# A squared-ReLU MLP on eight cores: the down projection as seven block products in place of eight, with sums shared in PSUM

## The chip, the cores and the metric

The kernel runs on all 8 cores of one Trainium2 chip, one sequence of the batch on each core, with no communication between them. The metric is the device time of the slowest core, in microseconds (us). Some executions fell in a second, slower state: some or all cores of one die show a lower granted clock than the others, and the time is longer.

A word on the names. TensorE multiplies (PE in the profile; PEld is its weight load), VectorE (DVE), ScalarE (ACT) and GpSimd (POOL) work on the elements, SyncE (SP) issues transfers. TensorE writes into PSUM, which the kernel uses as eight banks of 128x512 fp32; its other tiles lie in SBUF. "L858" is line 858 of that kernel's source, and one source line keeps its meaning in all kernels, though its number moves.

## The reference, cut to what matters

```python
D_MODEL = 1024; BATCH = 8; SEQ = 2048; D_FF = 4 * D_MODEL
...
        # token-mixing sub-layer: attention in two groups of heads, with a rotary key (k_pe)
        h = rmsnorm(x, norm_mix_g[l]) * (1.0 + sc1) + sh1
        ...
        x = x + g1 * jnp.einsum('bse,ed->bsd', mix, w_o[l])
        # channel-mixing sub-layer: squared-ReLU MLP
        h = rmsnorm(x, norm_mlp_g[l]) * (1.0 + sc2) + sh2
        u = jnp.square(jax.nn.relu(jnp.einsum('bsd,df->bsf', h, w_up[l])))
        x = x + g2 * jnp.einsum('bsf,fd->bsd', u, w_down[l])
    return rmsnorm(x, final_g)
```

The last einsum is the down projection: 2048 tokens by 4096 hidden features by 1024 outputs on each core.

## The kernel before

The kernel records operations with the buffers that they read and write. Its own scheduler then puts them in an order for each engine, places the PSUM tiles in banks and adds the semaphores. So the order of the source isn't the order on the engine.

The MLP runs over 4 quarters `q` of the hidden width and 4 groups `G` of 512 tokens, 16 blocks in all. The up matmuls of the next block are recorded ahead of the down matmuls of this one:

```python
        def mm_group(out, bank, lhs_list, rhs_list, rbufs):
            n = len(lhs_list)
            for i in range(n):
                S.op("pe", lambda h, i=i: h.matmul(out, lhsT=lhs_list[i], rhs=rhs_list[i], start=(i == 0), stop=(i == n - 1)),
                     r=rbufs[i], w=[bankb[bank]])
...
        def load_dn(q, after=()):           # down weights: load fp32, scale by the gate, store bf16
            ...
                S.op("dve", lambda h, c=c, w_=w_: h.tensor_tensor(out=WDN[s_][:, c, :], in0=WST[w_], in1=G2B, op=ALU.mult),
                     r=[bWST[w_], bG2], w=[bWDN[s_][c]])
...
        def mlp_up(q, G, fcs=range(8), banks=(0, 1, 2, 3)):
            for fc in fcs:
                ...                         # 8 matmuls into one bank
                if (q == 0 and G < 2) or (q == 3 and fc % 2):
                    S.op("dve", ...tensor_scalar(out=RT[rs], in0=bk(b), scalar1=0.0, scalar2=None, op0=ALU.max)...)
                    S.op("pool", ...tensor_tensor(out=UT[us][:, fc, :], in0=RT[rs], in1=RT[rs], op=ALU.mult)...)
                else:
                    S.op("act", ...activation(out=RT[rs], in_=bk(b), func=AF.Relu)...)
                    S.op("act", ...activation(out=UT[us][:, fc, :], in_=RT[rs], func=AF.Square)...)
...
        def mlp_down(q, G):
            ...
            for j in range(4):              # 4 token tiles of the group
                t = G * 4 + j
                for half in range(2):       # 2 x 512 output features
                    b = take_bank((4, 5, 6, 7))
                    mm_group(bk(b), b, [UT[us][:, fc, j * 128:(j + 1) * 128] for fc in range(8)],
                             [WDN[s_][:, fc, half * 512:(half + 1) * 512] for fc in range(8)],
                             [[bUT[us][fc], bWDN[s_][fc]] for fc in range(8)])
                    ...                     # VectorE: X1[t] += bank (a copy in the first quarter)
```

Two small pieces of the earlier stage are touched as well. The rotary key is copied to 8 heads by DMA, and eight scalings of two columns are VectorE instructions:

```python
            S.op("dve", lambda h: h.tensor_tensor(out=KPE, in0=TQ[0:32, :], in1=TQ[32:64, :], op=ALU.add), r=[bTQ], w=[bKPE])
            for r0 in (64, 96):
                S.dma("sp", lambda h, r0=r0: h.dma_start(out=KG[G][r0:r0 + 32, :, :],
                                                         in_=KPE.unsqueeze(1).to_broadcast([32, 8, 512])), ...)
...
        def scale_cols(i, src, c):          # (1 + MODCOL) * gain, 128x2
            S.op("dve", lambda h: h.scalar_tensor_tensor(out=GCOLS[:, i, 2 * c:2 * c + 2], ..., scalar=1.0, ..., op0=ALU.add, op1=ALU.mult),
                 r=[bMOD[src // 2 + c], bPAR], w=[bGC[i][c]])
```

The softmax here doesn't subtract the row's maximum and nothing guards it: scores larger than these inputs give would overflow.

## Time and profile before

| kernel before | |
|---|---|
| time, first three runs | 868.8 us (867.95 to 871.31) |
| slowest core of the profiled run | 873.4 us |
| TensorE busy there | 800.3 us in 5674 matmuls |
| VectorE, ScalarE, GpSimd busy | 391.8, 412.7, 194.0 us |
| from 0 to 442 us (projections, attention, start of the MLP) | TensorE idle for 64 us |
| from 442 to 862 us (the rest of the MLP) | TensorE idle for 0 us |

How to read it: the busy share of TensorE, 92%, mixes two stages. In the second one only the number of matmuls counts. In the first, TensorE waits for others, and a matmul saved there may be worth nothing. The prediction shows the lines and works with them.

### The profile page before, as it was taken

The numbers are of one execution on the slowest core, as the hardware profiler recorded it, in microseconds if no ns is written. First come the engines' busy times: TensorE is split into PE (matmuls) and PEld (weight loads), VectorE is DVE, ScalarE is ACT, GpSimd is POOL, SyncE is SP. The second block draws the span as 40 slices with busy tenths as digits, with TensorE's granted clock in tenths as the row PEclk, the third lists the DMA queues.
The fourth block names the chain that finished last, engine by engine and source line by source line (L and its number), as shares of the span: only waits on it lengthen the run. The fifth ranks groups of instructions, "written<-read, shape, count | busy, mean of one in ns | idle before, by whom it ended". The sixth has DMA issues, their size and how long they took to land.

```text
span 873.4 us, 16095 instructions; the slowest of 8 cores (854.4 to 873.4 us)
## 1 busy us (share of the span) xinstructions
PE 800.3 (92%) x5674; PEld 412.3 (47%) x5674; DVE 391.8 (45%) x684; ACT 412.7 (47%) x670; POOL 194.0 (22%) x164
## 2 busy tenths in 40 slices
PE   0697978899999988997999999999999999999995
PEld 0353546566556655554444444444444444444442
DVE  2575635844543436665662222512215344325546
ACT  3328627467789895770204323442234322124434
POOL 2020127557954443100170000000000000111110
PEclk9998989999999998999999999999999999999999
DMA  9999761579214355886571050600505321002213
GB/s 183 239 157 181 153 140 39 112 134 196 69 26 168 112 170 128 238 277 205 144 173 46 1 96 1 188 6 1 97 1 168 121 97 49 1 1 96 82 64 144
DMA packets 34301, 98.33 MB, mean 113 GB/s; under 512 B 3376, under 2 KB 9648, under 8 KB 34096
## 3 DMA queue, kind: packets, MB, share of 16 engines
q1 hardware_dynamic: 26016, 69.91, 24.6%
q0 software_dynamic: 8208, 27.40, 19.5%
q8 instruction: 47, 0.77, 0.4%
q14 instruction: 30, 0.25, 0.1%
HBM read 102.67 MB, written 19.92 MB: 140 GB/s over the span
## 4 chain that ended last, share of the span: by engine, by line
PE 79%; DMA 10%; issue 3%; ACT 3%; DVE 3%; POOL 1%; SPq 0%; DVEq 0%; ACTq 0%; POOLq 0%
PE ps L844 64%; PE ps L1225 6%; DMA arena<-wada 4%; PE ps L1249 3%; DMA arena<-arena 3%; DMA arena<-wdn 2%; DMA arena<-x 1%; PE ps L1271 1%; PE ps L1296 1%; PE ps L936 1%; PE ps L1333 1%; ACT arena L1058 1%; ACT arena L1233 1%; DMA mxs<-arena 1%; PE ps L1413 1%
## 5 line engine op out<-in xcount | busy, mean ns | idle before, releaser
L844 PE MATMUL ps<-arena 128*128 128x512 bf16 (+3 forms) x3444 | 676.1, 346 | 47.2 <-DMA arena<-wada 22.5
L844 PEld LDWEIGHTS ps<-arena 128*128 128x128 bf16 (+1 forms) x3444 | 298.3, 98 | 372.3 <-issue 68.2
L1472 ACT ACTIVATE arena<-ps 128x512 f32<-128x512 f32 x96 | 57.4, 598 | 250.8 <-PE ps L844 250.5
L1233 ACT ACTIVATE arena<-ps 128x1024 bf16<-128x1024 f32 (+1 forms) x160 | 138.8, 897 | 57.8 <-PE ps L1249 28.6
L1603 DVE TENSOR_TENSOR arena<-ps,arena 128x512 f32<-128x512 f32 x104 | 70.9, 689 | 150.8 <-PE ps L844 150.5
L1225 PE MATMUL ps<-arena 128*128 128x512 bf16 (+3 forms) x416 | 88.4, 310 | 4.8 <-ACT arena L1233 3.3
L911 ACT ACTIVATE arena<-arena 128x1024 bf16<-128x1024 f32 x47 | 49.6, 1055 | 87.9 <-DVE arena L1603 35.5
L1469 POOL TENSOR_TENSOR arena<-arena 128x512 bf16<-128x512 f32 x32 | 35.2, 1111 | 251.5 <-DVE arena L1467 243.1
L1278 POOL TENSOR_TENSOR arena<-arena 128x1024 bf16<-128x1024 f32 x31 | 73.0, 2354 | 62.5 <-ACT arena L1275 34.4
L1249 PEld LDWEIGHTS ps<-arena 128*128 128x128 bf16 x1088 | 54.1, 98 | 27.6 <-issue 6.7
L1249 PE MATMUL ps<-arena 128*128 128x65 bf16 x1088 | 63.8, 195 | 3.6 <-DVE arena L1310 2.9
L1474 ACT ACTIVATE arena<-arena 128x512 bf16<-128x512 f32 x96 | 60.6, 631 | 9.4 <-ACT arena L1472 0.9
L1238 POOL TENSOR_TENSOR arena<-arena 128x512 bf16<-128x512 bf16 x32 | 37.9, 1184 | 72.6 <-ACT arena L1233 57.8
L1445 DVE TENSOR_TENSOR arena<-arena 128x1024 bf16<-128x1024 f32 x32 | 40.6, 1275 | 27.4 <-DMA arena<-wdn 26.9
L1435 POOL DMA_DIRECT2D arena<-wup x16 | 9.1, 578 | 169.7 <-PE ps L844 169.7
L1225 PEld LDWEIGHTS ps<-arena 128*128 128x128 bf16 x416 | 32.1, 99 | 25.1 <-issue 16.2
L1467 DVE TENSOR_SCALAR arena<-ps 128x512 f32<-128x512 f32 x32 | 21.9, 690 | 46.9 <-PE ps L844 42.4
L1600 DVE COPY arena<-ps 128x512 f32<-128x512 f32 x24 | 16.4, 689 | 46.4 <-PE ps L844 46.4
L1387 DVE TENSOR_TENSOR arena<-ps,arena 128x512 f32<-128x512 f32 x32 | 22.0, 688 | 31.1 <-PE ps L844 18.9
L1275 ACT ACTIVATE arena<-ps 128x1024 f32<-128x1024 f32 x31 | 31.7, 1024 | 7.4 <-PE ps L844 1.8
L868 POOL DMA_DIRECT2D arena<-wada x24 | 13.6, 571 | 87.5 <-PE ps L844 45.7
L1353 DVE TENSOR_TENSOR arena<-ps,arena 128x512 bf16<-128x512 f32 x32 | 21.9, 688 | 21.2 <-PE ps L844 12.9
(83 smaller groups left out, 460.9 us busy)
## 6 DMA issues: line engine op xcount, KB each, us to landing
arena<-x SPq DMA_DIRECT2D x32, 512.0 KB, 9.0
arena<-wdn SPq DMA_DIRECT2D x32, 512.0 KB, 4.5
arena<-wada POOLq DMA_DIRECT2D x24, 512.0 KB, 11.0
arena<-wup POOLq DMA_DIRECT2D x16, 512.0 KB, 7.2
out<-arena SPq DMA_DIRECT2D x15, 512.0 KB, 2.6
x1s<-arena SPq DMA_DIRECT2D x12, 512.0 KB, 5.0
arena<-x1s SPq DMA_DIRECT2D x12, 512.0 KB, 3.2
mxs<-arena SPq DMA_DIRECT2D x12, 256.0 KB, 2.2
```

The source lines that it names most:

```text
L844: S.op("pe", lambda h, i=i: h.matmul(out, lhsT=lhs_list[i], rhs=rhs_list[i], start=(i == 0), stop=(i == n - 1)), r=rbufs[i], w=[bankb[bank]])
L911: S.op("act", lambda h: h.activation(out=dst, in_=src, func=AF.Square, accum_out=STA[st][:, j:j + 1]), r=[bsrc], w=[bSTA[st][j], bdst])
L1225: S.op("pe", lambda h, c=c, j=j, q0=q0, n=n: h.matmul(score(t)[:, c:c + n], lhsT=KG[j // 4][:, hh, j % 4 * 128:j % 4 * 128 + 128], rhs=QG[ ...
L1233: S.op("act", lambda h: h.activation(out=PT[p][:, 0:n], in_=score(t)[:, 0:n], func=AF.Exp, scale=MLA_SCALE), r=[t.buf], w=[bPT[p]])
L1238: S.op("pool", lambda h: h.tensor_tensor(out=v, in0=v, in1=TRI.unsqueeze(1).to_broadcast([128, m, 128]), op=ALU.mult), r=[bPT[p], bTRI], w ...
L1249: sp=(self.last and i == len(blocks) - 1): h.matmul(bk(ob, None, (qb * 65, qb * 65 + 65)), lhsT=PT[p][:, c:c + 128], rhs=vaug(j, hh), star ...
L1278: S.op("pool", lambda h: h.tensor_tensor(out=PTS[ps], in0=PE32[p], in1=EM[:, idx, :].rearrange("p (a b) -> p a b", a=2, b=512), op=ALU.mul ...
L1445: S.op("dve", lambda h, c=c, w_=w_: h.tensor_tensor(out=WDN[s_][:, c, :], in0=WST[w_], in1=G2B, op=ALU.mult), r=[bWST[w_], bG2], w=[bWDN[s ...
L1469: S.op("pool", lambda h, rs=rs, fc=fc: h.tensor_tensor(out=UT[us][:, fc, :], in0=RT[rs], in1=RT[rs], op=ALU.mult), r=[bRT[rs]], w=[bUT[us] ...
L1472: S.op("act", lambda h, b=b, rs=rs: h.activation(out=RT[rs], in_=bk(b), func=AF.Relu), r=[bankb[b]], w=[bRT[rs]])
L1474: S.op("act", lambda h, rs=rs, fc=fc: h.activation(out=UT[us][:, fc, :], in_=RT[rs], func=AF.Square), r=[bRT[rs]], w=[bUT[us][fc]])
L1603: S.op("dve", lambda h, t=t, hs=hs, b=b: h.tensor_tensor(out=X1[t][:, hs], in0=bk(b), in1=X1[t][:, hs], op=ALU.add), r=[bankb[b], bX1[t]], ...
```

## The change

The intent: the down projection of a block, 512 tokens by 1024 hidden by 1024 outputs, is cut in 2x2 blocks on all three sides. Strassen's scheme (in Winograd's form, with shared sums) takes 7 block products in place of 8, for four sums of activation blocks and four sums of weight blocks. The products that several output blocks share add up in one PSUM bank: product 1 is read out (for output block 00), 6 is accumulated upon it and the sum read (01), then 7 (11), then 4 (10). So 14 readings serve a block.

```diff
+        def sub(d, a, b, op=ALU.subtract):
+            S.op("dve", lambda h: h.tensor_tensor(out=d[0], in0=a[0], in1=b[0], op=op), r=a[1] + b[1], w=d[1])
+        def t_comb(q):                      # 4 sums of weight blocks, once a quarter
+            sub(WT[0], B[0, 1], B[0, 0]); sub(WT[2], B[1, 1], B[0, 1]); sub(WT[1], B[1, 1], WT[0]); sub(WT[3], B[1, 0], WT[1])
+        def s_comb(i):                      # 4 sums of activation blocks, in each of 15 blocks
+            sub(USB[0], A[1, 0], A[1, 1], ALU.add); sub(USB[2], A[0, 0], A[1, 0]); sub(USB[1], USB[0], A[0, 0]); sub(USB[3], A[0, 1], USB[1])
...
         def mlp_down(q, G):
+            ...                             # q == 3 and G == 3: as before, 64 matmuls
+            prods = {1: (u_blk(us, 0, 0), B[0, 0]), 2: (u_blk(us, 0, 1), B[1, 0]), 3: (USB[3], B[1, 1]),
+                     4: (u_blk(us, 1, 1), WT[3]), 5: (USB[0], WT[0]), 6: (USB[1], WT[1]), 7: (USB[2], WT[2])}
+            chain = {1: "a", 6: "a", 7: "a", 4: "a", 5: "b", 3: "b", 2: "c"}
+            to = {1: (0, 0), 6: (0, 1), 7: (1, 1), 4: (1, 0), 5: (1, 1), 3: (0, 1), 2: (0, 0)}
+            for p, n in ((0, 1), (0, 5), (1, 1), (0, 6), (1, 5), (0, 2), (1, 6), (0, 7), (0, 3), (1, 2), (1, 7), (0, 4), (1, 3), (1, 4)):
+                key = (p, chain[n])
+                first = key not in banks    # a bank for each chain of each half
+                ...
+                for f in range(4):
+                    S.op("pe", ...matmul(bk(b), lhsT=av[:, f, ...], rhs=wv[:, f, :], start=(first and f == 0), stop=(f == 3))...)
+                r, half = to[n]
+                acc(q, 4 * G + p + 2 * r, half, b)      # VectorE: X1 += bank
```

Two companions come with it in the earlier stage. For the first two groups the rotary key is copied by VectorE in place of the DMA; and four of the eight column scalings go to GpSimd as two instructions each (computed as m*g + g):

```diff
+            if G < 2:
+                for r0 in (64, 96):
+                    S.op("dve", ...tensor_copy(out=KG[G][r0:r0 + 32, :, :], in_=KPE.unsqueeze(1).to_broadcast([32, 8, 512]))...)
+                return
...
+            if i == 0:
+                S.op("dve", ...scalar_tensor_tensor...)     # as before
+            else:
+                S.op("pool", ...tensor_tensor(out=gc, in0=mc, in1=g, op=ALU.mult)...)
+                S.op("pool", ...tensor_tensor(out=gc, in0=gc, in1=g, op=ALU.add)...)
```

The rest makes room: the down weights lie in four blocks and are scaled in halves of 512 columns, output tiles are tracked by halves, and the scratch for DMA descriptors is halved. Two smaller things move as well: the matmuls of the MLP's loop may take any of the eight banks (before, up and down had four each), and the gain of the last normalisation is loaded later.

## The prediction

> **What bounds the kernel now.** I read the page first, then the chain of waits in order of time, then busy time by windows, then the rows of single instructions. The page's first part says that TensorE is busy for 92% of the span and nothing else for more than half:
>
> ```profile
> PE 800.3 (92%) x5674; PEld 412.3 (47%) x5674; DVE 391.8 (45%) x684; ACT 412.7 (47%) x670; POOL 194.0 (22%) x164
> ```
>
> That share is an average over two different stages. The chain of waits has one piece that is nearly half of the span (start, length, what, how many instructions):
>
> ```profile
> 442.39 419.32 PE ps L844 x1942
> ```
>
> The windows, cut at that piece's ends (the columns are the stretch, its length, busy time with instruction counts of PE, PEld, DVE, ACT and POOL, then the granted clock, the DMA share and GB/s):
>
> ```profile
> 0.00:442.39 442.39, 378.35 (x3720) 221.17 (x3721) 231.10 (x482) 268.14 (x411) 161.28 (x129) 0.97 0.65 154
> 442.39:861.90 419.51, 419.51 (x1944) 190.29 (x1945) 154.42 (x195) 140.30 (x248) 32.73 (x35) 1.00 0.23 68
> 861.90:873.40 11.50, 2.39 (x12) 0.88 (x9) 6.29 (x9) 4.29 (x11) 0.00 (x0) 0.83 0.34 138
> ```
>
> From 442.39 to 861.90 us, the MLP, TensorE never stops: 419.51 busy of 419.51, at full clock. 419.32 us over 1942 matmuls is 0.2159 us each. Nothing but fewer matmuls can shorten this stage, and each one taken away is worth 0.216 us as long as no wait takes its place. VectorE works for 37% of it (154.42 of 419.51), so there is room for more work beside it. The stage before is another matter: TensorE idles 64 of 442 us there, and two of the idle stretches are touched by this change. The waits ahead of TensorE (in brackets: idle before, and who ended it), and the VectorE row behind the second:
>
> ```profile
> 122.80 1.04 PE L844 MATMUL ps<-arena 128*128 128x512 bf16 x3 [5.06 <-DVE arena L1047]
> 155.47 0.90 PE L844 MATMUL ps<-arena 128*128 128x512 bf16 x3 [4.26 <-DVE arena L940]
> 150.63 4.29 DVE L899 SCALAR_TENSOR_TENSOR arena<-arena 128x2 f32<-128x2 f32 x1
> 151.45 2.35 POOL L1278 TENSOR_TENSOR arena<-arena 128x1024 bf16<-128x1024 f32 x1
> ```
>
> The first comes from a copy of the rotary key by DMA: the chain has 23.77 us of "DMA arena<-arena" from 97.38 us on, and VectorE sits 10.3 us behind it. The second is an instruction on two columns that takes 4.29 us instead of its median of 0.16, beside a GpSimd instruction.
>
> [...] after the idle 5.06 us the granted clock reads 0.50 from 122 to 128 us, and 0.57 from 156 to 160. [...] 689 ns for the 512-column accumulation out of PSUM[...], 1226 ns for the median 1024-column fp32 scaling[...]. No bf16 SBUF-only addition runs on VectorE before the change[...]. [...]
>
> **The change part by part.**
>
> *Matmuls removed.* The down projection is 4 quarters of the hidden width by 4 groups of 512 tokens, 16 blocks of 64 matmuls. Fifteen become 7 products of 8 matmuls, 56; the last stays at 64. 15 x 8 = 120 fewer, x 0.2159 = **25.9 us**, all of it on the path. This is 2.98% of 868.8.
>
> *Readings added.* Each product is added from PSUM into its output tile while the bank goes on accumulating: 14 readings of 128x512 in a block where there were 8. 15 x 6 = 90 more at 0.689 = 62 us of VectorE.
>
> *Sums of blocks added.* Per Strassen block four sums of 128x1024 bf16 of the activations: 60 at an estimated [...] 0.69 us[...] = 41 us. Per quarter four sums of 128x2048 of the weights: 16 at 1.22 = 20 us. The scaling of the down weights is cut in halves, 64 at 0.69 in place of 32 at 1.23 to 1.27: +4 us. Together VectorE gains 127 us, and in the MLP goes from 154 to some 280 of 394 us, 71%. So VectorE doesn't become the bound by its sum.
>
> *Does it fit in time?* One step of the steady state is 64 up matmuls (13.8 us) and 56 down (12.1 us). In the 12.1 us VectorE has 14 x 0.69 = 9.7 us of readings. The listing of VectorE's order shows the sums for the next block standing between them: with all four, 12.4 us of work in 12.1. What doesn't fit runs on into the 13.8 us of up matmuls, where VectorE has little to do. A single bank is tighter. A product takes 4 x 0.216 = 0.86 us, and a bank is written again after two other products at the least, 1.73 us. The reading needs a semaphore each way (0.14 us between VectorE and TensorE in the chain at 122.66) and 0.69: about 1.0. That leaves 0.75 us: one activation sum ahead of the reading fits (0.69), a weight sum (1.22) makes TensorE wait 0.5. In five of the 15 blocks the listing of TensorE's order puts two up matmuls ahead of the last product, which fills 0.43 us of just such a wait. In each of the three blocks that end a quarter two weight sums stand between the readings, the others behind them: 6 x 0.5 = 3 us at most, some of it hidden where the bank read next has more room, and some lost elsewhere to queueing. I charge **+2.5** for the stage.
>
> *The start of the MLP.* From 420 to 470 us VectorE gains the first four weight sums (4.9), four activation sums (2.8), the split scalings and a dozen readings (8), and in the same stretch GpSimd squares the activations[...]. Before, TensorE already waits 1.6 us for those squares at 441. I charge **+4**.
>
> *The early stage.* For the first two groups the rotary copy moves from DMA to VectorE, where it is a few us of work in a stretch in which VectorE waits; the later four of the eight small column scalings move to GpSimd[...]. What can come back is 5.06 idle plus half of some 5.7 us at half clock (2.9), and 4.26 plus 0.43 x 4 = 1.7: 13.9 us. The instructions behind then meet the next limit, so I take less than half: **-6**. The halved descriptor scratch is needed for the space and I give it nothing.
>
> *The end.* The last block is unchanged and the 11.5 us after the last matmul hold the same chain; four output tiles of the group before are finished together and late: **+0.5**.
>
> Sum: 868.8 - 25.9 - 6 + 4 + 2.5 + 0.5 = 843.9.
>
> **The rivals.** *VectorE paces the down blocks.* For it: 12.4 us of work in 12.1 with the sums, 19 with the weight sums, a queue in strict order, and readings queued behind scalings that wait for a DMA (26.9 us of such waits in all now). Against it: the readings have 0.75 us of slack, and 13.8 us of up matmuls after each block take up what is left over. If each of 15 blocks lost 1 us more, 859, within 2%. *The early stage gives nothing*, because the DMA queue or ScalarE bounds it (ScalarE is busy 45.3 of 50 us from 250 on): 850, just beyond 2%. *The early stage gives all*: 836. *The clock falls under the denser work*: the MLP reads 1.00 throughout and TensorE is no denser than before; I leave it out. *Accumulating and reading in one bank serialises*: if every product waited for its own reading, 15 x 14 x 0.3 us or more, 63 us slower; the three chains of banks per half speak against it.
>
> **Range and chances.** The 25.9 is a count by a measured time and is firm to 1 us. The early stage is open by +6 or -6, the stalls from 0 to +10. Together 844, from 835 to 854 in 8 of 10. Faster by over 2% means under 851.4: 0.86. Slower needs over 40 us of new waits: 0.01.
>
> **What would show it.** In the changed profile: 1824 or so matmuls between the start of the dense piece and its end; if the step of 0.216 us holds, that piece lasts some 394 us, with waits of TensorE for VectorE below 5 us in sum and mostly in the blocks that end a quarter. Activation sums near 0.69 and weight sums near 1.22 us; VectorE near 280 us in the MLP. The 5.06 and 4.26 us waits gone, and the MLP starting some 6 us earlier than 442. I am wrong if TensorE has many waits near 0.5 us on the accumulation,[...] or if the idle time of the early stage only moves.

The forecast's sum came to 868.8 - 25.9 - 6 + 4 + 2.5 + 0.5 = 843.9. Its terms +4 and +2.5, and 61 of the 127 us of VectorE's gain, rest in part on 0.69 us for an activation sum (128x1024 bf16) and 1.22 us for a weight sum (128x2048). These were the assumption; the trace of the kernel before has no such sum. The changed kernel's trace has means of 0.708 and 1.214 us.

## The result, and the profile after

| | before | after |
|---|---|---|
| median | 870.05 us (867.95 to 871.64, 4 runs) | 839.88 us (838.73 to 841.27, 4 runs) |
| ratio, 95% interval | | 0.9655 (0.9624 to 0.9686) |

A ratio here is the mean time of one kernel's fast runs over that of the other's fast runs of the same rounds, so it isn't quite the ratio of the medians. 3.45% of 870.05 is 30.0 us. The point of the prediction, 844.0, was 4 us too high; the time lies in its range. The results of this kernel and of all that follow were correct.

The engines' busy line of the changed kernel, from its page (which is of core 0, 836.1 us; the views below are of core 3, 836.8 us):

```profile
PE 770.8 (92%) x5554; PEld 397.0 (47%) x5554; DVE 504.9 (60%) x882; ACT 409.7 (49%) x670; POOL 200.8 (24%) x172
```

The counts are those of the plan: 5674 - 5554 = 120 matmuls fewer, VectorE with 113 us more work (127 by the prediction's sum of durations). The chain of waits in the middle of the MLP of the changed kernel (core 3, span 836.8 us; start, length, what, how many):

```profile
464.14 12.09 PE ps L1682 x56
476.23 13.81 PE ps L858 x64
```

The chain runs through TensorE alone, here and in the blocks that follow: 56 matmuls of a down block (L1682) take 12.09 us, so 0.2159 us each, and the 64 up matmuls (L858) follow without a gap. The windows of the changed kernel, with the columns of the prediction's table; the first ends at the start of the MLP, the third is its even part:

```profile
0.00:408.40 408.40, 359.17 (x3653) 211.38 (x3654) 218.50 (x474) 267.77 (x411) 156.22 (x131) 0.98 0.65 153
408.40:463.00 54.60, 48.94 (x221) 21.34 (x219) 45.07 (x62) 7.86 (x13) 21.68 (x18) 0.97 0.54 141
463.00:814.00 351.00, 350.40 (x1623) 158.40 (x1622) 224.78 (x327) 122.95 (x216) 22.72 (x24) 1.00 0.22 65
```

In the third window TensorE is busy 350.40 of 351.00 us at a clock of 1.00, though VectorE now works 64% of the time there. The second window is the sore point: VectorE 45.07 of 54.60 us, TensorE idle for 5.7. The waits of TensorE behind the last transpose ahead of the MLP, which starts at 427.3 us in the kernel before and at 408.4 us in the changed one (who it waited for; us in sum, times, the longest), first of the kernel before, then of the changed one, core 3 of both:

```profile
PE ps L844 <- POOL arena L1469: 1.6, 1, 1.6
```

```profile
PE ps L1682 <- DVE arena L1607: 2.6, 1, 2.6
PE ps L1682 <- DVE arena L1643: 1.8, 1, 1.8
PE ps L1682 <- POOL arena L1495: 1.2, 1, 1.2
PE ps L1682 <- DVE arena L1645: 0.6, 2, 0.4
```

L1607 is a sum of blocks, L1643 and L1645 are readings of a bank (the first as a copy), L1495 is GpSimd's squares. In the changed kernel they come to 6.2 us on this core and to 6.9 to 9.3 us on the others. The first three all stand between 409 and 444 us: 5.6 to 7.3 us by core, 6.6 in the mean, where the kernel before has 0 to 1.6 us, 0.3 in the mean. The readings of the whole even part cost 0.6 us on this core and 0.3 to 2.0 on the others. So nearly all of the 120 matmuls turned into time, except at the start of the MLP.

### The profile page after: what moved, and what is told of

Its sections match the earlier page's. It is cut to its first block, busy times and chain, and to the rows that moved or that the text cites. A ratio compares the mean times of both kernels' runs of the same rounds, so it can differ in the third digit from the quotient of the medians.

```text
span 836.1 us, 16205 instructions; the slowest of 8 cores (829.1 to 836.8 us)
## 1 busy us (share of the span) xinstructions
PE 770.8 (92%) x5554; PEld 397.0 (47%) x5554; DVE 504.9 (60%) x882; ACT 409.7 (49%) x670; POOL 200.8 (24%) x172
## 3 DMA queue, kind: packets, MB, share of 16 engines
q1 hardware_dynamic: 24928, 68.87, 24.9%
## 4 chain that ended last, share of the span: by engine, by line
PE 81%; DMA 7%; DVE 4%; issue 3%; ACT 3%; POOL 1%; SPq 0%; DVEq 0%; ACTq 0%; POOLq 0%
PE ps L858 45%; PE ps L1682 21%; PE ps L1248 7%; PE ps L1272 4%; DMA arena<-winl 3%; DMA arena<-wdn 2%; PE ps L1294 1%; DMA arena<-x 1%; DMA arena<-wada 1%; PE ps L1319 1%; PE ps L1356 1%; DVE arena L1470 1%; PE ps L1436 1%; ACT arena L1256 1%; DVE arena L1645 1%
## 5 line engine op out<-in xcount | busy, mean ns | idle before, releaser
L858 PE MATMUL ps<-arena 128*128 128x512 bf16 (+3 forms) x2484 | 468.6, 331 | 29.8 <-DMA arena<-wada 21.7
L858 PEld LDWEIGHTS ps<-arena 128*128 128x128 bf16 (+1 forms) x2484 | 203.6, 98 | 240.3 <-issue 47.1
L1682 PE MATMUL ps<-arena 128*128 128x512 bf16 x840 | 188.4, 381 | 7.8 <-DVE arena L1643 3.3
L1645 DVE TENSOR_TENSOR arena<-ps,arena 128x512 f32<-128x512 f32 x194 | 127.3, 685 | 76.9 <-PE ps L1682 73.6
L1256 ACT ACTIVATE arena<-ps 128x1024 bf16<-128x1024 f32 (+1 forms) x160 | 138.5, 895 | 43.2 <-PE ps L1272 18.9
L1682 PEld LDWEIGHTS ps<-arena 128*128 128x128 bf16 x840 | 82.1, 98 | 109.2 <-issue 13.1
L1495 POOL TENSOR_TENSOR arena<-arena 128x512 bf16<-128x512 f32 x32 | 40.5, 1270 | 236.9 <-PE ps L858 125.2
L1248 PE MATMUL ps<-arena 128*128 128x512 bf16 (+3 forms) x416 | 87.7, 306 | 6.6 <-ACT arena L1256 4.9
L1272 PE MATMUL ps<-arena 128*128 128x65 bf16 x1088 | 65.7, 193 | 1.3 <-DVE arena L1282 0.3
L1272 PEld LDWEIGHTS ps<-arena 128*128 128x128 bf16 x1088 | 54.3, 97 | 25.3 <-issue 4.4
L1607 DVE TENSOR_TENSOR arena<-arena 128x1024 bf16<-128x1024 bf16 (+1 forms) x76 | 61.0, 815 | 0.6
L1470 DVE TENSOR_TENSOR arena<-arena 128x512 bf16<-128x512 f32 x64 | 48.2, 789 | 13.5 <-DMA arena<-wdn 10.9
L1248 PEld LDWEIGHTS ps<-arena 128*128 128x128 bf16 x416 | 31.6, 97 | 25.8 <-issue 16.9
L1410 DVE TENSOR_TENSOR arena<-ps,arena 128x512 f32<-128x512 f32 x32 | 22.0, 689 | 32.7 <-PE ps L858 15.0
L1298 ACT ACTIVATE arena<-ps 128x1024 f32<-128x1024 f32 x31 | 31.7, 1023 | 10.5 <-POOL arena L1301 3.8
```

The source lines that it names most:

```text
L1248: S.op("pe", lambda h, c=c, j=j, q0=q0, n=n: h.matmul(score(t)[:, c:c + n], lhsT=KG[j // 4][:, hh, j % 4 * 128:j % 4 * 128 + 128], rhs=QG[ ...
L1256: S.op("act", lambda h: h.activation(out=PT[p][:, 0:n], in_=score(t)[:, 0:n], func=AF.Exp, scale=MLA_SCALE), r=[t.buf], w=[bPT[p]])
L1272: sp=(self.last and i == len(blocks) - 1): h.matmul(bk(ob, None, (qb * 65, qb * 65 + 65)), lhsT=PT[p][:, c:c + 128], rhs=vaug(j, hh), star ...
L1470: S.op("dve", lambda h, c=c, w_=w_, n=n, v=v: h.tensor_tensor(out=v[:, c % 4, :], in0=WST[w_][:, n * 512:n * 512 + 512], in1=G2B[:, n * 51 ...
L1607: S.op("dve", lambda h: h.tensor_tensor(out=d[0], in0=a[0], in1=b[0], op=op), r=a[1] + b[1], w=d[1])
L1645: S.op("dve", lambda h: h.tensor_tensor(out=X1[t][:, hs], in0=bk(b), in1=X1[t][:, hs], op=ALU.add), r=[bankb[b], bX1[t][half]], w=[bX1[t][ ...
```

## The experiments

Twelve kernels ran in three batches, each batch on one chip with the kernel before beside it. The questions: (a) how the gain divides between the matmuls and the two companions; (b) why TensorE waits at the start of the MLP; (c) how near VectorE is to becoming the bound; (d) what the sharing of banks and the order of products are worth.

### (a) Companions and matmuls apart

**early_only** is the kernel before with both companions, **rope_only** and **scale_only** have one each, and **strassen_only** is the changed kernel with both taken back:

```diff
 # strassen_only, against the changed kernel
-            if G < 2:
-                ...tensor_copy(out=KG[G]...)   # back to the DMA
-                S.op("pool", ...)              # scale_cols: back to VectorE
```

> The kernel before with the two companions alone (rotary copy of groups 0 and 1 by VectorE, the second set of column scalings on GpSimd), no Strassen. Theory A, from the two traces: the companions bring 12 to 15 us, because the last transpose ahead of the MLP ends 14.5 us earlier in the median core; expects 855 to 858, ratio near 0.984. Theory B: the earlier mark is work that moved, and Strassen alone brings the whole 30 us; expects 866 to 870, ratio 0.995 to 1.0.

> The changed kernel with both companions put back (rotary copies by DMA, all column scalings on VectorE). Theory A: 25.9 us of matmuls less some 8 of waits at the start of the MLP, 17 to 19 us; expects 851 to 853, ratio near 0.980. Theory B: 840 to 843, ratio near 0.967.

> The kernel before with the rotary copy of groups 0 and 1 by VectorE alone. Theory A: takes the 5.1 us wait of TensorE at 122.8 and the half-speed clock behind it, 7 to 9 us; expects 861 to 863. Rival: the attention starts earlier but meets the stuck column scaling, which then costs more; expects 866 to 870.

> The kernel before with the second set of column scalings on GpSimd alone. Theory A: takes the 4.3 us wait at 155.5 and its clock loss, 5 to 6 us; expects 864 to 866. Rival: the 4.29 us instruction was slow in this one profile by chance, nothing comes back; expects 869 to 871.

| kernel | median | ratio to before (95%) | about |
|---|---|---|---|
| early_only | 860.84 us | 0.9879 (0.9860 to 0.9898) | -10.5 us |
| strassen_only | 852.32 us | 0.9763 (0.9729 to 0.9796) | -20.6 us |
| rope_only | 867.78 us | 0.9961 (0.9942 to 0.9979) | -3.4 us |
| scale_only | 864.74 us | 0.9916 (0.9892 to 0.9940) | -7.3 us |

(us: one minus the ratio, times 870. The median of strassen_only is over six runs of which two were slow; its fast runs lie from 848.16 to 854.64. early_only and scale_only had one slow run each.) The parts multiply: 0.9879 x 0.9763 = 0.9645 against 0.9655 for the whole change, and 0.9961 x 0.9916 = 0.9877 against 0.9879. By the expectations, strassen_only and scale_only came out as theory A says, rope_only in its rival's range, and early_only between its two theories.

So a third of the gain isn't Strassen's. The waits of TensorE between 100 and 300 us suggest why the smaller companion gave more. The three longest entries of the kernel before, then those of rope_only, scale_only and early_only that are over 2 us (for the last, which has none, its longest):

```profile
PE ps L844 <- DVE arena L1047: 5.1, 1, 5.1
PE ps L844 <- DVE arena L940: 4.3, 1, 4.3
PE ps L844 <- DVE arena L1336: 1.2, 1, 1.2
```

```profile
PE ps L844 <- DVE arena L940: 4.3, 1, 4.3
PE ps L844 <- DVE arena L1341: 2.1, 1, 2.1
```

```profile
PE ps L844 <- DVE arena L1051: 3.4, 1, 3.4
```

```profile
PE ps L1234 <- ACT arena L1242: 1.4, 4, 0.8
```

The rotary wait (L1047, L1051) goes with the first companion, but the wait behind the scalings (L940) stays and another (L1341) grows by 0.9: 10.6 - 6.4 = 4.2 us less, 3.4 measured. The second companion takes L940 away, and the rotary wait shrinks with it from 5.1 to 3.4, presumably since VectorE comes to its work earlier: 10.6 - 3.4 = 7.2 less, 7.3 measured. With both the three are gone: 10.6 less, 10.5 measured. Each sum is one profile of one core, so the agreement to tenths is luck, and it leaves out two things: a later wait of the same kind (L1336, at 397 to 401 us, 4.4 us on this core of the kernel before; 3.7 on that of early_only), and the slower clock behind the waits (0.50 from 122 to 128 us and 0.57 from 156 to 160 in the kernel before), to which the prediction gave 4.6 us. That scale_only gains more than rope_only rests on their times.

What stands beside an instruction on two columns that holds VectorE for 4.29 us is seen on GpSimd's timeline (kernel before; the VectorE row, L899 from 150.63 to 154.92, is in the prediction):

```profile
149.73 1.18 POOL L1238 TENSOR_TENSOR arena<-arena 128x512 bf16<-128x512 bf16 x1
150.83 0.59 POOL L868 DMA_DIRECT2D arena<-wada  x1
151.45 2.35 POOL L1278 TENSOR_TENSOR arena<-arena 128x1024 bf16<-128x1024 f32 x1
153.75 1.15 POOL L1238 TENSOR_TENSOR arena<-arena 128x512 bf16<-128x512 bf16 x1
```

It starts within the first of three GpSimd operations on two tensors (after the first of them GpSimd issues a DMA) and ends with the end of the third, at 154.90. In this stretch the two engines didn't take turns: VectorE's row ends only where GpSimd pauses (GpSimd's next instruction starts at 159.53). Given to GpSimd itself, the scaling is two instructions of 0.2 us each (medians of 202 and 190 ns in early_only).

### (b) The start of the MLP

Two theories for the waits there. A: the squares on GpSimd and the two-input work of VectorE block each other. B: VectorE simply has too much to do. Two kernels, both the changed one with an edit in the up projection:

```diff
 # squares_on_act: in quarter 0 only the squares move from GpSimd to ScalarE
-                    S.op("pool", ...tensor_tensor(out=UT..., in0=RT[rs], in1=RT[rs], op=ALU.mult)...)
+                    S.op("act", ...activation(out=UT..., in_=RT[rs], func=AF.Square)...)   # if q == 0
 # relu_squares_on_act: maximum and squares of quarter 0 move to ScalarE
-                if (q == 0 and G < 2) or (q == 3 and fc % 2):
+                if q == 3 and fc % 2:
```

> The changed kernel with the squares of the first two MLP steps on ScalarE in place of GpSimd; VectorE keeps its relus, so its own work is the same. Theory A: the 7 us of TensorE waits between 408 and 445 us come from VectorE instructions with two SBUF inputs and GpSimd squares blocking each other (two scalings took 2.66 us beside a square, 1.28 without); expects 834 to 837, and scalings and sums at 0.68 us throughout. Rival: VectorE simply has too much work there (45 of 54.6 us); expects 838 to 840.

> The same with relus and squares both on ScalarE, which also takes 11 us of work off VectorE in that stretch. Theory A (blocking alone): the same as the run with squares alone, 834 to 837. Rival (VectorE's load): better than it by 3 us or more, 831 to 834. It may be worse if ScalarE is still busy with the last exponentials.

squares_on_act: 0.9557 of the kernel before (0.9522 to 0.9592; fast runs of 831.96, 832.82 and 835.89 us, two slow). relu_squares_on_act: **830.84 us** (830.62 to 833.31, 4 runs), 0.9532 (0.9506 to 0.9558). Against 0.9655 for the change these are some 8.5 and 10.7 us more gain, and the second beats both kernels. By the expectations, squares_on_act is in the range of theory A, and relu_squares_on_act beats it by 2.2 us, where the rival asked for 3 or more. The windows from 400 to 455 us of the slowest core of each, before, after, squares_on_act, relu_squares_on_act (the first isn't the same work: up to 427 us the kernel before is still in the stage ahead of the MLP):

```profile
400.00:455.00 55.00, 50.63 (x267) 24.09 (x268) 34.65 (x53) 5.84 (x16) 18.47 (x20) 0.97 0.64 172
```

```profile
400.00:455.00 55.00, 48.54 (x237) 21.78 (x236) 52.62 (x72) 6.41 (x20) 23.31 (x19) 0.97 0.58 149
```

```profile
400.00:455.00 55.00, 53.39 (x269) 24.66 (x268) 44.39 (x71) 20.55 (x41) 2.19 (x4) 1.00 0.56 149
```

```profile
400.00:455.00 55.00, 54.27 (x275) 25.33 (x273) 35.35 (x55) 29.73 (x58) 2.19 (x4) 1.00 0.56 149
```

In the changed kernel VectorE is busy 52.62 of 55 us there, the most of any stretch, while ScalarE has 6.41 us of work. Taking GpSimd's squares away saves VectorE 8 us for all but the same number of instructions (72 and 71), because they get shorter. The scalings of the down weights in the changed kernel and in relu_squares_on_act (ns: least, median, most):

```profile
L1470 DVE TENSOR_TENSOR arena<-arena x64: 674/685/1529, 324.3 to 652.8; 128x512 bf16<-128x512 f32 x64
```

```profile
L1470 DVE TENSOR_TENSOR arena<-arena x64: 681/685/693, 322.9 to 644.8; 128x512 bf16<-128x512 f32 x64
```

The same instruction takes up to 1529 ns beside the squares and at most 693 ns without them; in the changed kernel, the 13 of them between 410 and 445 us have a median of 1210 ns. From 408 to 450 us of the changed kernel (core 3) the other rows beside the squares show how far this goes. Activation sums, which like the scalings read two tiles in SBUF, take up to 1522 ns (median of all 684), and the squares themselves up to 1886, with a median of 1414 (from 714 to 804 us it is 1039). The 13 maximum instructions (673 to 692 ns) and the copies out of a bank (673 to 678), with one input from PSUM, stay as they are, and so do the weight sums at 1.21 us. So the blocking of A is shown for scalings, activation sums and squares, with some 8 us of VectorE's time, and taking the squares off GpSimd brings most of the gain. The load of B is worth no more than the rest, some 2 us between the two kernels, within their intervals. What these runs don't separate from the blocking is the squares' own length: on GpSimd they have a median of 1.04 us, on ScalarE of 0.63; one wait of TensorE, 1.2 us, was on them directly, and one of VectorE, 1.0 us.

Or is ScalarE the better place whatever the down projection does? **before_act** is the kernel before with the edit of relu_squares_on_act:

> The kernel before, with the same edit as in the fastest version so far: maximum and squares of the first two steps of the MLP on ScalarE instead of VectorE and GpSimd. In the changed kernel this edit gave some 10 us. Theory A: it gave them because the change had loaded VectorE and GpSimd at the start of the MLP (waits of TensorE of 6.5 to 8.8 us there, 0 to 1.6 us in the kernel before); then it is worth 0 to 3 us here: 867 to 871 us. Theory B: ScalarE is the better place whatever the down projection does, and the edit has nothing to do with the change: then 860 to 863 us here, too.

870.05 us (the median of four; 867.57 to 870.46 in its three fast runs), as theory A says; ratio 0.9952 (0.9879 to 1.0025). The interval is wide, as the kernel before had runs from 868.67 to 880.09 in this batch that count as fast. It allows anything from 2 us lost to 10 us gained, so the times alone don't exclude theory B of its expectation, though its middle, 4 us, is well below 10.7 us. (The run of 880.09 us has cores 0 and 1 at a clock of 0.95, as slow runs do; without it the middle is 2.5 us.) Its profile says more: before_act has 0.9 us of waits of TensorE in the MLP where the kernel before has 1.6 at most, so there was little to gain.

### (c) Is VectorE near its limit?

**sums_twice** computes the four activation sums of 14 blocks a second time, 56 x 0.69 = 39 us more of VectorE (34.0 in the profile, 538.9 against 504.9):

```diff
+            if i > 0:
+                sub(USB[0], A[1, 0], A[1, 1], ALU.add) ... # the four sums once more
```

> The changed kernel with the four activation sums of 14 blocks computed twice, 2.8 us more of VectorE a block, the same result. Theory A: the up matmuls (13.8 us a step) take up what VectorE has left over, so the time stays within 4 us of 840. Rival (VectorE paces the down blocks: 12.4 us of work in 12.1, now 15.2): 14 times 2.8 us, 875 to 880.

841.65 us, fast runs from 838.61 to 843.49, ratio 0.9621 (0.9586 to 0.9656) where the change has 0.9655: no cost that the times show, as theory A says. The window of its even part:

```profile
463.00:814.00 351.00, 347.35 (x1608) 156.72 (x1606) 251.99 (x373) 121.64 (x214) 26.81 (x24) 1.00 0.22 65
```

VectorE is at 72% and TensorE still at 99% (it idles for 3.65 us there, against 0.60 in the changed kernel). So the activation sums, a third of what the change adds to VectorE, were hidden with room to spare. **unshared** goes further: each product has its own bank and is added into each output block from there, 28 readings a block in place of 14:

```diff
-                key = (p, chain[n])
+                key = (p, n)
...
-                r, half = to[n]
-                acc(q, 4 * G + p + 2 * r, half, b)
+                for r, half in into[n]:     # 1: 4 blocks, 6: 3, 7: 2, 5: 2, 4, 3, 2: 1 each
+                    acc(q, 4 * G + p + 2 * r, half, b)
```

> The changed kernel, but every product has a PSUM bank of its own, and each is added into every output block that it belongs to straight from there: the 14 readings of a block become 2 x (4 + 3 + 1 + 2 + 1 + 1 = 12) = 24 or a few more, in place of 14; TensorE's work is the same. What is the sharing of sums in PSUM worth? Theory A: VectorE becomes the bound of the MLP. It is busy about 225 + 45 = 270 us of the some 405 us behind 408 us in the changed kernel; 15 blocks x at least 10 more readings x 0.69 us = 104 us or more give 375 to 415 us, in a queue of strict order, so TensorE must wait: 860 to 890 us, with waits of TensorE for readings throughout the MLP, 25 us or more in sum. Theory B, a rival: VectorE's sum still is under the stage's length and the waits stay hidden behind the up matmuls: 840 to 848 us.

(The expectation's count of readings was wrong: 2 x 14 = 28, not 24.) 871.56 us (870.35 to 873.75, 4 runs), ratio 0.9987 (0.9914 to 1.0060): all of the gain is gone, some 30 us of it against the changed kernel, in the range of theory A. Its window behind the start of the MLP, and the longest of its waits of TensorE from 410 us on:

```profile
463.00:850.00 387.00, 365.63 (x1647) 160.62 (x1646) 336.04 (x526) 122.28 (x218) 23.63 (x24) 0.97 0.21 59
```

```profile
PE ps L1684 <- DVE arena L1645: 16.6, 10, 4.0
PE ps L858 <- DVE arena L1645: 6.2, 13, 0.5
```

VectorE is busy 87% of the stretch, and TensorE waits 22.8 us for readings: 0.5 us ahead of 13 runs of up matmuls, and up to 4.0 us at the end of a quarter, where the weight sums and the scalings, which wait for their DMA, stand ahead of readings in VectorE's queue. TensorE has the same matmuls as in the changed kernel, but they take 779.6 us in place of 770.8, as its clock reads 0.97 in this stretch and not 1.00: waits and clock together are about the 30 us. What unshared doesn't separate is VectorE's load from the banks: each product now holds a bank of its own for up to four readings. Sharing the sums in PSUM saves 15 x 14 = 210 readings, 113.9 us of VectorE's busy time over the run (618.8 against 504.9), and without it the seven products gain nothing. (210 x 0.68 would be 143 us. Readings that follow one another overlap in the record, with starts some 0.60 us apart, so a sum of durations overstates.)

### (d) What the order of products is worth

The kernel records each product and each reading on the buffer of its bank, so its scheduler makes an accumulation onto a bank wait for the reading before it (113 such waits, 121.5 us in sum, in forced_same_bank below). The source interleaves two halves with three banks each to hide this. **same_bank_next** put the products of one half in a row instead:

```diff
-            for p, n in ((0, 1), (0, 5), (1, 1), (0, 6), (1, 5), ...):
+            for p, n in [(p, n) for p in range(2) for n in (1, 6, 7, 4, 5, 3, 2)]:
```

> The changed kernel with the products ordered so that a bank is written again right after its own product (1, 6, 7, 4, 5, 3, 2 for one half of the tokens, then the other). Theory A: each of the 4 returns to a bank per half waits for a reading, 1.0 us, 8 a block, 15 blocks: some 100 us slower, 920 to 960, with TensorE waits on the accumulation of near 1 us each. Rival: TensorE finds other matmuls to do or the waits are hidden; 840 to 860.

It took 837.06 us in one run, no longer than the changed kernel, a plain miss for theory A. Its profile has 2.2 us of waits for readings in the MLP and single up matmuls between the products, so the engine's order wasn't the source's. A listing of TensorE's order showed that the scheduler had interleaved the halves and banks by itself. The edit hadn't done what its name says. The mended pair ties each MLP matmul to the one recorded before it. **forced_interleaved** is the control, **forced_same_bank** has the products in a row:

```diff
+                for o in S.all[n0:]:
+                    if o.eng == "pe":
+                        if pe_prev:
+                            o.deps.append((pe_prev[-1], 0, "order"))
+                        pe_prev.append(o)
```

> The changed kernel, but TensorE's order in the MLP is fixed to the order of the source (64 up matmuls, then 56 of the down block with the products of the two halves and three chains of banks interleaved as the author wrote them), so that the scheduler can't put other matmuls in between. It is the control for the next kernel. Where the interleaving leaves at least two other products between two uses of a bank (1.73 us against about 1.0 us for a reading with its semaphores), nothing waits: 838 to 845 us. If the order hides too little, waits near 0.5 us show up on the first matmul of products: 845 to 860 us.

> As the control, with fixed order, but the products of one half in a row: 1, 6, 7, 4 in one bank, 5, 3 in another, 2 in a third. Theory A (accumulating and reading in one bank serialise unless other products lie between): each of the 15 x 2 x 4 = 120 returns to the bank just written waits for the reading of 0.69 us and a semaphore each way, about 1.0 us: 120 us more than the control, some 960 us, with waits of about 1.0 us on the accumulation. Theory B: the reading overlaps with the next product in the same bank, or the wait is much shorter: less than 20 us more than the control.

One execution each (theory A of the second one names 960 us): 837.75 us and **1021.2 us**. Both profiled runs were fast, with the two dies alike. The waits of TensorE from 410 us on, control first:

```profile
PE ps L1682 <- DVE arena L1607: 2.6, 1, 2.6
PE ps L1682 <- DVE arena L1643: 1.8, 1, 1.8
PE ps L1682 <- DVE arena L1645: 1.3, 3, 0.5
```

```profile
PE ps L1682 <- DVE arena L1645: 109.1, 100, 2.8
PE ps L1682 <- DVE arena L1643: 12.4, 13, 1.1
```

In the row-wise order 113 waits for readings take 121.5 us, near the expectation's 120 returns of 1.0 us. The chain shows one of them in its parts, a product, its reading, the semaphore, the next product in the same bank:

```profile
697.61 1.04 PE ps L1682 x4
698.74 0.70 DVE arena L1645
699.45 0.14 issue
699.58 1.04 PE ps L1682 x4
```

But the time rose by 183 us, not by 120. The windows over the same block show the other 60 (columns as in the prediction's table; the clock is the third number from the right):

```profile
695.80:700.00 4.20, 2.31 (x11) 0.74 (x9) 1.38 (x2) 1.23 (x2) 0.00 (x0) 1.00 0.00 0
700.00:704.00 4.00, 2.49 (x11) 0.81 (x9) 1.77 (x3) 0.00 (x0) 0.00 (x0) 1.00 0.00 0
704.00:708.00 4.00, 2.75 (x12) 1.10 (x12) 2.55 (x5) 0.00 (x0) 0.00 (x0) 1.00 0.00 0
708.00:712.00 4.00, 2.58 (x8) 0.75 (x8) 1.62 (x3) 0.00 (x0) 0.00 (x0) 0.79 0.00 0
712.00:716.00 4.00, 3.06 (x8) 1.05 (x8) 3.12 (x4) 0.00 (x0) 0.00 (x0) 0.50 0.00 0
```

From 695.8 to 708 TensorE is busy for 7.55 of 12.2 us, and none of its waits there is longer than 1.3 us. Then the clock falls to half, and 8 matmuls fill 3.06 us where they took 1.7. Over the whole run TensorE is busy 835.1 us, 64.4 more than the control's 770.7, for the same 5554 matmuls. 120 and 64 make up the 183. Here, then, the waits cost half as much again as their own length. The order hides nearly all of it: in the author's order TensorE waits 3.1 us for readings.

## Why the prediction was right

**Matmuls, -25.9 us: right.** 120 fewer, at 0.216 us in the chain, with no wait in the place of the removed ones. strassen_only, the change without its companions, gave -20.6 (-17.7 to -23.6); the prediction's terms for it are -25.9 + 4 + 2.5 + 0.5 = -18.9.

**The early stage, -6: the mechanism was right, the size too small.** The two waits went as named, and the companions gave 10.5 us of the 13.9 held recoverable. The step that was off is "I take less than half": it charged for a next limit, and 10.5 of 13.9 came back. Nor were the two parts weighed rightly. The prediction gave 8.0 of the 13.9 to the rotary copy and 6.0 to the scalings; alone they brought 3.4 and 7.3, presumably since the scalings also held up the rotary work and the rotary copy left the 4.3 us wait behind it in place.

**The start of the MLP, +4: the place was right, the size too small.** TensorE waits there for 5.6 to 7.3 us by core where it waited 0 to 1.6, so about +6 in the mean. The prediction named the added VectorE work and GpSimd's squares side by side; squares_on_act shows that the squares' place is the larger part.

**Stalls in the even part, +2.5: too large.** TensorE idles 0.6 of 351 us on core 3, and its waits for readings there are 0.3 to 2.0 us by core. In place of six stalls of 0.5 us there are one to three, most of them shorter. The up matmuls slotted in between aren't needed for that: forced_interleaved, which has none, waits 1.3 us in three stalls. (The "19" us of a down block with the weight sums doesn't follow from the prediction's own terms: 12.4 and four times 1.22 are 17.3.)

**The end, +0.5: nothing to see.** From the last matmul to the end it is 9 us in both kernels. (The prediction's 11.5 us "after the last matmul" still hold 12 matmuls.)

The sum with the measured terms is -25.9 - 10.5 + 6 + 0.6 = -29.8, against -30.0 measured and -24.9 predicted. The 5 us between are 4.5 (early stage) - 2 (start of the MLP) + 1.9 (even part) + 0.5 (end): errors of both signs, so that the point came within 4 us is in part luck. The terms come from ratios and single profiles, so the 0.2 us that are left are luck, too.

**The assumed durations of the sums held.** Activation sums (1024 columns) have a mean of 708 ns (assumed 690) and weight sums (2048 columns) of 1214 (assumed 1220). No trace of the kernel before showed them; that they held is measured in the changed kernel alone. VectorE's sum grew by 113 us and not by 127; readings that overlap in the record, as in (c), are the likely reason.

**The rivals.** "VectorE paces the down blocks" is refuted by sums_twice, and unshared shows how far off it was: it comes true with 114 us more (and with the banks held longer). "The early stage gives nothing" is refuted by early_only, and "gives all" was nearer the truth than the -6. "The clock falls" didn't happen in the changed kernel (1.00 in the even part). "Accumulating and reading in one bank serialises" is true of the forced order, at 183 us rather than the 63 that the prediction put on it, and is what the interleaving of chains avoids.

**What stays open.** The halved scratch for DMA descriptors was never tried alone; it is in strassen_only, so whatever it does is in those 20.6 us. The same holds for the eight banks that up and down matmuls now share, and for the later load of the last gain. How far the squares' own length adds to the blocking at the start of the MLP wasn't separated either.

## What to carry to other kernels

Where TensorE is the bound and runs gapless, as here, a matmul saved was worth its full time (0.216 us) wherever what replaced it on another engine stayed within that engine's slack in the stretch itself, and not only on average; that meant halving the readings by accumulating in PSUM (871.56 us without it, in unshared), and spacing the uses of a bank (1021.2 us without it, in forced_same_bank). After such a change, look for the one stretch where the engine that took the work is full while another is idle: moving the maximum and squares of two steps from VectorE and GpSimd to ScalarE gave another 10 us. And take companions of a change apart: a third of this gain came from two small edits outside of the MLP.

## What the traces show of the hardware

- The granted clock fell to half or near it in two settings. In the kernel before (core 3) it reads 0.50 from 122 to 128 us, behind a wait of TensorE of 5.06 us, and 0.57 from 156 to 160, behind one of 4.26. In forced_same_bank it fell to 0.50 (712 to 716 us) with TensorE 62% busy (7.55 of 12.2 us) and no wait over 1.3 us in the stretch ahead of it. How much idling it takes isn't fixed by these runs.
- All eight cores of the changed kernel ran dense matmuls from 463 to 814 us at a granted clock of 1.00, with means of 0.985 to 0.991 over the profiled run. One slow execution of early_only had 0.813 to 0.814 on the four cores of one die (994.5 us); other slow ones lay from 0.86 upward.
- VectorE and GpSimd lengthened each other's instructions here. A 128x2 instruction of VectorE, 0.16 us by itself, lasted until three GpSimd instructions in a row had ended (4.29 us); a 0.685 us scaling took up to 1.53 us beside the squares, and a 1.04 us square up to 1.89.
- Going back to a bank that VectorE has just read cost 0.94 us between two products in forced_same_bank: 0.70 for the reading of 128x512, the rest for semaphores each way.
